# A two-layer hybrid decoder trunk: runs of sixteen products in the conv and gate projections, a later start of the second heads, and another room for the gated values

## The chip, the cores and the metric

The kernel runs on one core of a Trainium2 chip, in one launch. The metric is device time in microseconds (us), the median of several runs. The engines' names are those of the profile: PE is the matrix engine (PEld its weight loads), ACT the scalar engine, DVE the vector engine, POOL the general-purpose engine, SP the engine that issues most of the DMA transfers.

## What is computed

Input x has 256 tokens of 2048 features, in float32. Two layers follow each other. Cut to what matters here:

```python
for l in range(2):
    h = _rmsnorm(x, attn_norm_g[l])
    q, k, v, gate_b, gate_c, conv_in = split(h @ w_in[l])   # six parts of 1024 columns
    q, k = rmsnorm per 64 columns, with gains
    attn = diff_attention(q, k, v)       # 8 heads, two softmaxes each, one bias table
    attn = _rmsnorm(attn, subln_g[l]) * (1.0 - lam_init)
    conv = gate_b * _short_conv(gate_c * conv_in, conv_w[l])  # causal, 3 taps
    x = x + concatenate([attn, conv]) @ w_out[l]
    hm = _rmsnorm(x, mlp_norm_g[l]) @ w_up[l]                 # 8192 columns
    x = x + square(relu(hm)) @ w_down[l]
```

## The kernel before

**Products in three terms.** Every float32 operand is split into a part that PE's fast float32 form holds ("hi") and the rest ("lo"). A product of two operands is hi times hi, hi times lo and lo times hi. Weights come from memory as raw tiles of 128 x 1024 numbers (512 KB). For each, ACT writes the hi copy (`whi`, line 302) and DVE subtracts it from the raw tile (`wlo`, line 303). Three hi and three lo buffers exist (`wpool`), and four raw buffers in each mixer (`rpool`). `Weights.take` (line 357) hands out the next tile and has the following three made. In the MLP the same is done for the up weights (`uhi`, `ulo`, lines 818 and 819), from raw tiles of 1 MB (`uraw`, line 811), of which `upool` holds four.

**The mixer of a layer** (line 716) issues PE's work in this order: for each half of the heads q, k and v (16 contraction steps each, `linear`, line 373, 96 products of 512 columns); then four times gate-C and conv-in (`gc`, `ci`), then four times gate-B (`gb`), each of 256 output columns, all by `linear_t`; then four chunks of the output projection (`o`).

**`linear_t`** (line 392) turns the operands round: the weights are PE's stationary side, and the activations, hi and lo side by side (512 columns), move. For one weight tile of four contraction steps it issues eight products of `whi` with 512 moving columns ("wide" below) and then eight of `wlo` with the 256 hi columns ("narrow"). Sixteen contraction steps are four tiles: 64 products, in eight runs of eight. `up_part` (line 944), which makes the MLP's hidden columns, works the same way; when it is called with both halves of the contraction (the tiles `upw` and `upc`) it issues sixteen wide products from two weight tiles and then sixteen narrow ones. Called with one half (tile `up`, the MLP's first columns) it issues eight and eight.

**Background work.** PE's instructions run in the order in which the program issues them. Work of other stages is put between the products by steps: `Background.tick` (line 78) is called after a number of products, and each piece waiting in it counts down and goes on when its count is over. `linear` steps after six products. `linear_t` steps whenever k is odd, which is after every four products: 16 steps in a call. The order on ACT, DVE, POOL and SP is laid down when the program is built, by a planner with its own model of times; some instructions are kept in program order (`late`).

**Attention** (line 584) is such a piece. Four heads make up a half. A head computes scores in two banks (`sc`, line 604, eight products), DVE adds the bias and takes the maximum (610), ACT exponentiates (619), DVE joins the two softmaxes (630). After 10 x pace steps PE transposes (`ptp`, 635), after 4 x pace more it multiplies with the values (`av`, 646 and 648). The next head begins 8 x pace steps after the one before. 12 x pace steps after the last head's `av` the result is transposed in two goes, two steps apart (`atp`, 677), and ACT and DVE move each go into the tile `cat` (681 and 682). pace is 1 for the first half of the heads and 2 for the second. The call at line 763 starts a half 3 + 6 x half steps after its v projection, so the second half begins 9 steps into the first `gc`. All of `sc`, `ptp`, `atp` and some other small tiles take turns in three PSUM banks (`ps`, tag "bank").

**Gate and rooms.** `gate` (line 709) joins the two parts of a `gb` accumulator, multiplies them with the convolution's result into `y`, a tile of the shared pool `nat` (six buffers), and splits `y` into `cat` (lines 705 and 706). The masked keys `kL`, 8 KB per partition, lie in the pool `biasp` beside the bias table (16 KB); they are last read by the last head's scores. The mixer's pools are given up at its end, and the MLP's pools take their place in memory, `upool` first (4 x 8 KB); its tiles can be loaded as soon as whatever lay there has been read for the last time.

Of the kernel before, what the change touches and what calls it, by code (L numbers as in the profile page):

```python
# [9 lines left out]
F32 = mybir.dt.float32  # L10
F32R = mybir.dt.float32r
# [4 lines left out]
P = 128  # L16
DEPTH = 2
D = 2048
S = 256
NT = S // P  # L20
AW = 1024
# [8 lines left out]
WC = 256  # L30
KG = 4
# [14 lines left out]
def bucket_selector():  # L46

    import numpy as np

    d = np.arange(REL) - (P - 1)  # L50
    exact = NB // 2
    n = np.maximum(d, exact).astype(np.float64)
    large = exact + (np.log(n / exact) / math.log(MAXD / exact) * (NB - exact)).astype(np.int64)
    b = np.where(d < exact, d, np.minimum(large, NB - 1))
    b = np.where(d < 0, NB, b)
    return (np.arange(NB + 1)[:, None] == b[None, :]).astype(np.float32)


class Background:
# [46 lines left out]
def trunk(ctx: ExitStack, tc: tile.TileContext, x, w_in, w_out, conv_w, q_norm_g, k_norm_g,  # L106
# [8 lines left out]
    nat = ctx.enter_context(tc.tile_pool(name="nat", bufs=6))  # L115
# [10 lines left out]
    def bank(name):  # L126
        return ps.tile([P, CH], F32, tag="bank", name=name)
# [4 lines left out]
    work = Background()  # L132
# [56 lines left out]
    def tap(l, i, k):  # L189
        j = (l * 3 + i) * (AW // P) + k  # L190
        return gains[:, j:j + 1]
# [82 lines left out]
    class Parts:  # L274


        def __init__(self, pool, tag, name):
            self.make = lambda: pool.tile([P, 2, KG, S], F32R, tag=tag, name=name)
            self.ap = None
            self.ready = False  # L280
# [111 lines left out]
    def linear_t(name, acts, weights):  # L392

        acc = mm.tile([P, 2, 2, S], F32, tag="mm2", name=name)
        nk = len(acts) * KG
        for k0 in range(0, nk, 4):
            hi, lo = weights.take()  # L400
            a = acts[k0 // KG]
            while not a.ready:
                work.tick()
            for part, wt in ((0, hi), (1, lo)):
                for k in range(k0, k0 + 4):
                    for f in range(2):
                        fs = slice(f * P, (f + 1) * P)
                        nc.tensor.matmul(  # L408
                            acc[:, f, 0] if part else acc[:, f], wt[:, k % 4, fs],
                            a.ap[:, 0, k % KG] if part else a.ap[:, :, k % KG],  # L410
                            start=(part == 0 and k == 0), stop=(part == 1 and k == nk - 1),
                            skip_group_check=True)
                    if k % 2:
                        work.tick()
        return acc

    def joined(acc, name):

        low = nat.tile([P, 2, S], F32, tag="wide", name=f"{name}l")
        nc.scalar.activation(low, acc[:, :, 1], AF.Copy)  # L420
        whole = nat.tile([P, 2, S], F32, tag="wide", name=f"{name}w")
        nc.vector.tensor_add(whole, acc[:, :, 0], low)
        return whole
# [266 lines left out]
    def conv(l, q, u, cv, norm):  # L690

        for i in range(2):
            k = q * 2 + i
            nc.scalar.activation(cv[:, k], u[:, i], AF.Copy, scale=tap(l, 2, k))
            for back in (1, 2):
                nc.vector.scalar_tensor_tensor(
                    cv[:, k, back:], u[:, i, :S - back], tap(l, 2 - back, k),
                    cv[:, k, back:], op0=ALU.mult, op1=ALU.add)
        pair = cv[:, q * 2:q * 2 + 2]
        nc.gpsimd.tensor_tensor(pair, pair, norm.bc(1), op=ALU.mult)  # L700
# [5 lines left out]
        nc.vector.tensor_sub(lo, value, hi.bitcast(F32))  # L706
        dst.ready = j == 1

    def gate(q, acc, cv, dst):
        g = joined(acc, f"gb{q}")  # L710
        y = nat.tile([P, 2, S], F32, tag="wide", name=f"y{q}")
        nc.vector.tensor_mul(y, g, cv[:, q * 2:q * 2 + 2])
        in_parts(dst, q % 2, y)


    def mixer(l, norm, loads):

        with ExitStack() as scope:
            biasp = scope.enter_context(tc.tile_pool(name="biasp", bufs=1))
            tmp = scope.enter_context(tc.tile_pool(name="tmp", bufs=3))  # L720
            rpool = scope.enter_context(tc.tile_pool(name="rpool", bufs=RAW))
            bpool = scope.enter_context(tc.tile_pool(name="bpool", bufs=8))
            weights = Weights(rpool)
            setup = None
            if l == 0:
                setup = setup_loads(bpool.tile([P, 2 * KG * S], F32, tag="b", name="setup"))
            for half in range(2):
                for part in range(3):
                    weights.straight(w_in[l], 0, D // P, part * AW + half * CH)
            for q in range(AW // WC):  # L730
                for part in (4, 5):
                    weights.turned(w_in[l], part * AW + q * WC)
            for q in range(AW // WC):
                weights.turned(w_in[l], 3 * AW + q * WC)
            for n in range(D // CH):
                weights.straight(w_out[l], 0, D // P, n * CH)
            loads(weights)

            bias = biasp.tile([P, 2 * NH, S], F32, tag="bias", name="bias")
            work.start(load_bias(l, bpool, bias, setup), 10)  # L740
            hT = norm.tiles
            cat = [Parts(bpool, "b", f"cat{l}{i}") for i in range(4)]
            work.start(norm.factors(), 1)
            kL = biasp.tile([P, 2, 4, S], F32R, tag="kL", name=f"kL{l}")
            for m, r in enumerate(HALF):
                nc.gpsimd.memset(kL[HALF[1 - m], m].bitcast(F32), 0.0)
            for half in range(2):
                h0 = 4 * half
                acc = linear(f"q{l}{half}", hT, weights)
                r = norm.r  # L750
                qT = bpool.tile([P, 2, 4, S], F32R, tag="b", name=f"qT{l}{half}")
                work.start(qk_norm(acc, r, q_parts(qT), q_gain[:, l:l + 1], f"q{l}{half}"))
                acc = linear(f"k{l}{half}", hT, weights)
                kT = bpool.tile([P, 2, 4, S], F32R, tag="b", name=f"kT{l}{half}")
                work.start(qk_norm(acc, r, k_parts(kT, kL), k_gain[:, l:l + 1], f"k{l}{half}"))
                acc = linear(f"v{l}{half}", hT, weights)
                v = bpool.tile([P, 2, NT, CH], F32R, tag="b", name=f"v{l}{half}")
                for t in range(NT):
                    nc.scalar.activation(v[:, 0, t], acc[:, t], AF.Copy, scale=r[:, t:t + 1])
                    nc.vector.scalar_tensor_tensor(v[:, 1, t], acc[:, t], r[:, t:t + 1],  # L760
                                                   v[:, 0, t].bitcast(F32),
                                                   op0=ALU.mult, op1=ALU.subtract)
                work.start(attention(l, qT, kT, kL, v, h0, cat[half], bias, tmp,
                                     1 + half), 3 + 6 * half)
            cv = bpool.tile([P, AW // P, S], F32, tag="b", name=f"cv{l}")
            for q in range(AW // WC):
                acc = linear_t(f"gc{l}{q}", hT, weights)
                u = joined(acc, f"gc{l}{q}")
                nc.gpsimd.tensor_tensor(u, u, norm.bc(2), op=ALU.mult)
                acc = linear_t(f"ci{l}{q}", hT, weights)  # L770
                i = joined(acc, f"ci{l}{q}")
                nc.vector.tensor_mul(u, i, u)
                conv(l, q, u, cv, norm)
            for q in range(AW // WC):
                acc = linear_t(f"gb{l}{q}", hT, weights)
                gate(q, acc, cv, cat[2 + q // 2])

            mnorm = Norm(1, l)
            for n in range(D // CH):
                acc = linear(f"o{l}{n}", cat, weights)  # L780
                for t in range(NT):
                    nc.vector.tensor_add(xs[n][:, t], acc[:, t], xs[n][:, t])
                work.start(mnorm.chunk(n, 2))
        return mnorm
# [5 lines left out]
    def mlp(l, mnorm, last):  # L790
# [3 lines left out]
        SEVEN = [i for i in SEVEN_AT if i < 2 * BLK]  # L794
        mT = mnorm.tiles
        with ExitStack() as scope:
            upool = scope.enter_context(tc.tile_pool(name="upool", bufs=4))
            fpool = scope.enter_context(tc.tile_pool(name="fpool", bufs=2))
            dpool = scope.enter_context(tc.tile_pool(name="dpool", bufs=3))
            spool = scope.enter_context(tc.tile_pool(name="spool", bufs=1))  # L800
# [3 lines left out]
            weights = Weights(upool)  # L804
# [197 lines left out]
            for i in range(NP):  # L1002
# [15 lines left out]
                for c in range(2):  # L1018
                    if i < LAG:
                        acc = bank("upw").rearrange("p (h s) -> p h s", h=2)  # L1020
                    else:
                        acc = column_bank()
# [10 lines left out]
                    if j >= 0 and c == 0:  # L1033
                        b11, b21, b22 = weights.take()
                        t1, t3 = weights.take()
                        f = fs[j]
# [5 lines left out]
                    elif j >= 0:  # L1042
                        t2, t4 = weights.take()
                        f = fs[j]
# [223 lines left out]
```

## Time and profile before

| | |
|---|---|
| median of 3 runs | 2133.45 us (2132.67 to 2133.55) |
| the profiled execution | 2133.02 us |
| its span, first to last instruction | 2131.2 us |
| granted clock of PE | 1.00 throughout |
| PE busy | 2125.1 us |
| DVE / ACT / POOL busy | 1693.9 / 1349.2 / 165.6 us |
| PE's products | 10925 |
| gc, ci, gb of layer 0 | from 156.06 us to 300.71 us |
| gc, ci, gb of layer 1 | begin about 1059 us later |

Times in the rows that follow are us from the start of the span. A timeline row has the start, how long it lasted, the engine, the source line, the operation, out<-in by the program's tile names, the shape (partitions x elements) and the number of instructions that were merged into it; products overlap in the pipe, so the pace is the distance of one row's start from the next one's, not the duration. A bracket at the end is idle time before the row and what ended it. A row of waits has the waiting engine and tile, what it waited for, us in total, times, longest us. A row of the chain has the start, us, and what. A row of DMA issues has the count, the size, and the median us from issue to landing. A row of windows has the stretch, its length, the busy time of PE, PEld, DVE, ACT and POOL with counts, the clock, the DMA engines' busy share and GB/s.

### The profile page before, as it was taken

The page shows a single profiled execution, that of the slowest core. Times are in us where ns is not written, and L with a number is a line of the kernel's source. Part 1 is how long each engine was busy: PE and PEld are TensorE (multiplying, and loading weights), DVE is VectorE, ACT ScalarE, POOL GpSimd, SP SyncE. Part 2 cuts the span into 40 slices and gives each one's busy share as a digit, 9 for nine tenths or more (in the row PEclk, how much of TensorE's full clock was granted, in tenths as well). Part 3 has the DMA queues.
Part 4 walks back from the last instruction along what each step waited for, and adds up shares of the span by engine and source line. Part 5 has one row for each costly group of instructions (what it writes and reads, how often), then busy time and mean ns, then how long its engine had stood idle before and what let it go on. Part 6 is the DMA issues. An engine that isn't in the chain of part 4 may idle for free.

```text
span 2131.2 us, 29207 instructions
## 1 busy us (share of the span) xinstructions
PE 2125.1 (100%) x10925; PEld 1818.4 (85%) x10925; DVE 1693.9 (79%) x2316; ACT 1349.2 (63%) x1776; POOL 165.6 (8%) x226
## 2 busy tenths in 40 slices
PE   9999999999999999999999999999999999999999
PEld 8888888888888888888888888888888888888887
DVE  6778655798888888798766786557988888888986
ACT  6666545677777777656565665446777777675654
POOL 3110100000000000011111101000000000000110
PEclk9999999999999999999999999999999999999999
DMA  8555766677777777788656558656877777777983
GB/s 271 178 166 167 252 193 187 206 252 229 230 236 229 233 235 229 255 297 287 216 170 182 163 162 264 188 178 211 259 231 233 232 235 229 236 229 259 319 297 112
DMA packets 298255, 476.01 MB, mean 223 GB/s; under 512 B 12708, under 2 KB 193782, under 8 KB 298113
## 3 DMA queue, kind: packets, MB, share of 16 engines
q1 hardware_dynamic: 269120, 406.76, 60.5%
q0 software_dynamic: 28800, 67.24, 10.1%
q8 instruction: 85, 1.39, 0.3%
q14 instruction: 58, 0.47, 0.1%
q10 hardware_dynamic: 192, 0.15, 0.0%
HBM read 440.52 MB, written 33.58 MB: 222 GB/s over the span
## 4 chain that ended last, share of the span: by engine, by line
PE 99%; ACT 1%; DVE 0%; issue 0%; DVEq 0%; ACTq 0%
PE upc L955 31%; PE pr L998 14%; PE dn L1079 8%; PE o L386 8%; PE ci L408 4%; PE gb L408 4%; PE k L386 4%; PE q L386 4%; PE v L386 4%; PE gc L408 4%; PE dn L1161 2%; PE dn L998 2%; PE pr1r L998 1%; PE pr0r L998 1%; PE up L955 1%; PE upw L955 1%
## 5 line engine op out<-in xcount | busy, mean ns | idle before, releaser
L303 DVE TENSOR_TENSOR wlo<-raw,whi 128x1024 fp32r<-128x1024 f32 x274 | 343.0, 1252 | 217.8 <-ACT whi L302 213.6
L302 ACT ACTIVATE whi<-raw 128x1024 fp32r<-128x1024 f32 x274 | 290.4, 1060 | 303.3 <-PE o L386 73.6
L955 PE MATMUL upc<-nT,uhi 128*128 128x512 f32 x1920 | 454.7, 389 | 0.0
L955 PEld LDWEIGHTS upc<-nT,uhi 128*128 128x128 f32 x1920 | 360.3, 188 | 74.7
L819 DVE TENSOR_TENSOR ulo<-uraw,uhi 128x1024 fp32r<-128x1024 f32 x256 | 311.9, 1222 | 119.1 <-ACT f L987 91.4
L818 ACT ACTIVATE uhi<-uraw 128x1024 fp32r<-128x1024 f32 x256 | 270.5, 1057 | 159.9 <-PE upc L955 137.5
L955 PEld LDWEIGHTS upc<-nT,ulo 128*128 128x128 f32 x1920 | 246.2, 191 | 9.3
L955 PE MATMUL upc<-nT,ulo 128*128 128x256 f32 x1920 | 249.1, 283 | 0.0
L1079 PE MATMUL dn<-whi,fb 128*128 128x512 f32 x528 | 166.1, 389 | 0.0
L386 PE MATMUL o<-whi,cat 128*128 128x512 f32 x512 | 159.5, 390 | 0.0
L302 ACT ACTIVATE whi<-uraw 128x1024 fp32r<-128x1024 f32 x66 | 70.1, 1062 | 94.0 <-PE dn L1079 77.5
L1079 PEld LDWEIGHTS dn<-whi,fb 128*128 128x128 f32 x528 | 99.1, 188 | 20.6
L844 ACT ACTIVATE b2h<-draw 128x1024 fp32r<-128x1024 f32 x81 | 85.9, 1061 | 45.9 <-PE pr L998 41.3
L386 PEld LDWEIGHTS o<-whi,cat 128*128 128x128 f32 x512 | 96.2, 188 | 19.7
L965 ACT ACTIVATE ev<-upc 128x512 f32<-128x512 f32 x120 | 72.0, 600 | 54.1 <-PE upc L955 54.1
L1079 PE MATMUL dn<-wlo,fb 128*128 128x512 f32 x264 | 102.7, 389 | 0.0
L303 DVE TENSOR_TENSOR wlo<-uraw,whi 128x1024 fp32r<-128x1024 f32 x66 | 80.7, 1223 | 24.8 <-ACT whi L302 24.5
L844 ACT ACTIVATE t24h<-t 128x1024 fp32r<-128x1024 f32 x81 | 86.2, 1064 | 22.2 <-PE pr L998 15.8
L845 DVE TENSOR_TENSOR b2l<-draw,b2h 128x1024 fp32r<-128x1024 f32 x81 | 98.5, 1217 | 1.7 <-ACT b2h L844 1.7
L845 DVE TENSOR_TENSOR t24l<-t,t24h 128x1024 fp32r<-128x1024 f32 x81 | 98.7, 1219 | 1.3
L386 PE MATMUL o<-wlo,cat 128*128 128x512 f32 x256 | 99.6, 389 | 0.0
L845 DVE TENSOR_TENSOR t13l<-t,t13h 128x1024 fp32r<-128x1024 f32 x81 | 98.7, 1219 | 1.1
(408 smaller groups left out, 4153.3 us busy)
## 6 DMA issues: line engine op xcount, KB each, us to landing
uraw<-in_w_up_dram SPq DMA_DIRECT2D x128, 1024.0 KB, 6.2
raw<-in_w_in_dram SPq DMA_DIRECT2D x191, 512.0 KB, 3.8
draw<-in_w_down_dram SPq DMA_DIRECT2D x170, 512.0 KB, 5.2
uraw<-in_w_down_dram SPq DMA_DIRECT2D x66, 512.0 KB, 5.3
raw<-in_w_out_dram SPq DMA_DIRECT2D x64, 512.0 KB, 3.6
hid0p<-f POOLq DMA_DIRECT2D x20, 512.0 KB, 3.6
raw<-in_w_down_dram SPq DMA_DIRECT2D x10, 1024.0 KB, 5.1
fb<-hid0p POOLq DMA_DIRECT2D x20, 512.0 KB, 7.4
```

The source lines that it names most:

```text
L302: pair = (nc.scalar.activation(hi, raw, AF.Copy), nc.vector.tensor_sub(lo, raw, hi.bitcast(F32)))
L303: nc.vector.tensor_sub(lo, raw, hi.bitcast(F32)))
L386: nc.tensor.matmul(acc[:, t], a.ap[:, pa, k % KG, t * P:(t + 1) * P], (hi, lo)[pw][:, j], start=(k == 0 and n == 0), stop=(k == nk - 1 and ...
L408: nc.tensor.matmul(acc[:, f, 0] if part else acc[:, f], wt[:, k % 4, fs], a.ap[:, 0, k % KG] if part else a.ap[:, :, k % KG], start=(part ...
L818: pair = (nc.scalar.activation(hi, src, AF.Copy), nc.vector.tensor_sub(lo, src, hi.bitcast(F32)))
L819: nc.vector.tensor_sub(lo, src, hi.bitcast(F32)))
L844: keep(nc.scalar.activation(hi, src, AF.Copy))
L845: keep(nc.vector.tensor_sub(lo, src, hi.bitcast(F32)))
L955: nc.tensor.matmul(acc[:, 0] if part else acc, wt[part][:, k], a.ap[:, 0, k % KG] if part else a.ap[:, :, k % KG], start=(part == 0 and kh ...
L965: nc.scalar.activation(ev, acc, AF.Copy)
L998: nc.tensor.matmul(prods[n], f[:, pa, a], b[pw], start=(start and m == 0), stop=(stop and m == 2))
L1079: nc.tensor.matmul(prods[p], f[:, pa, 2 * k + t], b[pw][:, n], start=(p in starts and k == 0 and m == 0), stop=(stop and k == 1 and m == 2))
```

## The change

Three things change, in one diff.

- `linear_t` takes two weight tiles at a time and issues sixteen wide products from their hi parts and then sixteen narrow ones from their lo parts. The steps stay at 16 a call, but in a pair of runs they now come after 2, 6, 8, 10, 14 and 16 wide products and after 8 and 16 narrow ones.
- The second half of the heads starts 12 steps after its v projection instead of 9.
- `kL` gets a pool of its own, `kpool`, placed behind `biasp` so that the bytes stay where they were. When the masked keys are done, a tile `ys` takes that room and holds the gated values of all four `gb` blocks. The MLP's `upool` becomes two pools of two buffers, `upa` and `upb`, used by turns, two tiles of each.

```diff
+class Turns:
+    def __init__(self, *pools):
+        self.pools, self.n = pools, 0
+
+    def tile(self, *args, **kw):
+        self.n += 1
+        return self.pools[(self.n - 1) // 2 % 2].tile(*args, **kw)
...
         nk = len(acts) * KG
-        for k0 in range(0, nk, 4):
-            hi, lo = weights.take()
-            a = acts[k0 // KG]
-            while not a.ready:
-                work.tick()
-            for part, wt in ((0, hi), (1, lo)):
-                for k in range(k0, k0 + 4):
+        for k0 in range(0, nk, 8):
+
+            tiles = [weights.take() for _ in range(2)]
+            for part in range(2):
+                for k in range(k0, k0 + 8):
+                    a = acts[k // KG]
+                    while not a.ready:
+                        work.tick()
+                    wt = tiles[(k - k0) // 4][part]
                     for f in range(2):
...
-                    if k % 2:
+                    if k % 4 == 3 or (part == 0 and k % 2 == 0):
                         work.tick()
...
-    def gate(q, acc, cv, dst):
+    def gate(q, acc, cv, dst, y):
         g = joined(acc, f"gb{q}")
-        y = nat.tile([P, 2, S], F32, tag="wide", name=f"y{q}")
...
             biasp = scope.enter_context(tc.tile_pool(name="biasp", bufs=1))
+            kpool = scope.enter_context(tc.tile_pool(name="kpool", bufs=1))
...
-            kL = biasp.tile([P, 2, 4, S], F32R, tag="kL", name=f"kL{l}")
+            kL = kpool.tile([P, 2, 4, S], F32R, tag="kL", name=f"kL{l}")
...
                 work.start(attention(l, qT, kT, kL, v, h0, cat[half], bias, tmp,
-                                     1 + half), 3 + 6 * half)
+                                     1 + half), 3 + 9 * half)
...
+            ys = kpool.tile([P, AW // WC, 2, S], F32, tag="kL", name="ys")
             for q in range(AW // WC):
                 acc = linear_t(f"gb{l}{q}", hT, weights)
-                gate(q, acc, cv, cat[2 + q // 2])
+                gate(q, acc, cv, cat[2 + q // 2], ys[:, q])
...
-            upool = scope.enter_context(tc.tile_pool(name="upool", bufs=4))
+            upool = Turns(scope.enter_context(tc.tile_pool(name="upa", bufs=2)),
+                          scope.enter_context(tc.tile_pool(name="upb", bufs=2)))
```

## The prediction

> **What bounds the kernel now.** First the page: which engine is busy, and who ends the chain.
>
> ```profile
> span 2131.2 us, 29207 instructions
> PE 2125.1 (100%) x10925; PEld 1818.4 (85%) x10925; DVE 1693.9 (79%) x2316; ACT 1349.2 (63%) x1776; POOL 165.6 (8%) x226
> PE 99%; ACT 1%; DVE 0%; issue 0%; DVEq 0%; ACTq 0%
> ```
>
> PE never rests and is 99% of the chain that ended last. So only two things can move the time: the spacing of PE's products, or an idle stretch that PE gets or loses. The second view, the waits of PE, lists all the idle time there is:
>
> ```profile
> PE sc L604 <- DVE cat L682: 1.2, 2, 0.6
> PE warm L160 <- DVE mhalf L152: 1.1, 1, 1.1
> ```
>
> The second line is the start of the program, which the change leaves alone. The first is one wait per layer. The third view, PE's timeline at the beginning of gate-C's first block (gc, layer 0), shows where it lies:
>
> ```profile
> 156.06 1.98 PE L408 MATMUL gc<-nT,whi 128*128 128x512 f32 x8
> 157.87 1.12 PE L408 MATMUL gc<-nT,wlo 128*128 128x256 f32 x8
> 158.82 1.09 PE L408 MATMUL gc<-nT,whi 128*128 128x512 f32 x4
> 159.75 0.60 PE L677 MATMUL atp<-ident,an 128*128 128x128 f32 x4
> 160.10 1.17 PE L408 MATMUL gc<-nT,whi 128*128 128x512 f32 x4
> 161.11 0.64 PE L408 MATMUL gc<-nT,wlo 128*128 128x256 f32 x4
> 161.59 0.60 PE L677 MATMUL atp<-ident,an 128*128 128x128 f32 x4
> 161.94 0.72 PE L408 MATMUL gc<-nT,wlo 128*128 128x256 f32 x4
> 162.50 1.09 PE L408 MATMUL gc<-nT,whi 128*128 128x512 f32 x4
> 163.43 0.22 PE L604 MATMUL sc<-kT,qT 128*128 128x128 f32 x1
> 164.26 0.38 PE L604 MATMUL sc<-kT,qT 128*128 128x256 f32 x1 [0.61 <-DVE cat L682]
> ...
> 165.18 1.09 PE L408 MATMUL gc<-nT,whi 128*128 128x512 f32 x4
> ```
>
> The two atp lines are the first heads' last transposes, put in at steps 5 and 7 of this block (a step, a tick of the code, now follows every four products). The second heads' scores begin at step 9. There are three score banks, so the second score product takes the bank of the first atp and waits until DVE has emptied it:
>
> ```profile
> 163.47 0.74 DVE L682 SCALAR_TENSOR_TENSOR cat<-atp,s_gain,cat 128x512 fp32r<-128x512 f32 x1
> 164.12 1.22 DVE L303 TENSOR_TENSOR wlo<-raw,whi 128x1024 fp32r<-128x1024 f32 x1
> ```
>
> It ends at 163.47 + 0.74 = 164.21 and PE goes on at 164.26; the line below it is DVE's part in making a weight tile.
>
> **Part 1: the second heads three steps later.** An undisturbed set of scores, one head later in the same layer:
>
> ```profile
> 176.37 0.39 PE L604 MATMUL sc<-kT,qT 128*128 128x128 f32 x2
> ...
> 177.28 1.07 PE L408 MATMUL ci<-nT,whi 128*128 128x512 f32 x4
> ```
>
> From first score to next gc or ci product: 177.28 - 176.37 = 0.91 us undisturbed, 165.18 - 163.43 = 1.75 at the first. The wait costs 0.84 us per layer (more than the 0.61 listed as idle, since what was in the pipe runs empty), 1.7 us for two. Does it go? The new step 12 stands ten wide products into the second run. From 156.06: fourteen wide products (3.2), atp (0.35), two wide (0.54) and eight narrow (0.95), atp (0.35), eight narrow (1.04), ten wide (2.3) make 164.8. The bank is free at 164.21 if ACT and DVE keep their order, so there is 0.6 us to spare. The second atp's bank is wanted only by the next head, 16 steps on. I take the whole 1.7; the ends are 0 (DVE does the eviction after the weight tile that follows it, 1.22 us later) and 1.7. What is late next: by the waits view, nothing; the other scores, transposes and value products show no wait now and keep their distances of 20 and 8 steps. The second heads end three steps later, at step 116 of the 192 that gc, ci and gb have, and their result is read only after those.
>
> **Part 2: runs of sixteen.** Each block (linear_t, 24 of them: gc, ci, gb, four each, two layers) issues 64 products as eight runs now, and as four after. Count and operands stay. What a change of run costs is read where both forms exist. In gb's first runs, and in upw, the MLP's first columns, which already go in sixteens:
>
> ```profile
> 255.86 2.00 PE L408 MATMUL gb<-nT,whi 128*128 128x512 f32 x8
> 257.70 1.11 PE L408 MATMUL gb<-nT,wlo 128*128 128x256 f32 x8
> ```
>
> ```profile
> 402.55 3.82 PE L955 MATMUL upw<-nT,uhi 128*128 128x512 f32 x16
> 406.20 2.08 PE L955 MATMUL upw<-nT,ulo 128*128 128x256 f32 x16
> 408.12 1.09 PE L955 MATMUL upw<-nT,uhi 128*128 128x512 f32 x4
> ```
>
> Start to start: eight wide 1.84, sixteen 3.65, so the second eight take 1.81: the first products of a wide run behind a narrow one are slower, 0.03 us in all. Narrow: eight take 0.95 (157.87 to 158.82 above), sixteen 1.92, which gives some 0.01 to 0.02 back. The chain has it without rounding:
>
> ```profile
> 256.02 44.69 PE gb L408 x256
> ...
> 402.71 11.13 PE upw L955 x64
> ...
> 422.16 5.54 PE upc L955 x32
> ```
>
> A block takes 44.69 / 4 = 11.17 us in eights and 11.13 in sixteens: 0.04 less, times 24 = 1.0 us. With the 5.54 of a pair of runs that follows other wide products it would be 0.09, times 24 = 2.2; 0 is the other end. I take 1.0, as upw alone has sixteens behind sixteens.
>
> The Trainium skill ("TensorE: Matmul & The Clock Gate", Back-to-back issue gap) gives the distance of two products as moving columns / 2.4 plus 2.5 ns, whatever went before, and by that the length of a run is worth nothing. The trace has 3.65 / 16 = 228 ns in long runs and 1.84 / 8 = 230 in short ones, where that rule has 216 in both: it doesn't hold here to the ns that this part is about. By it the sum below would be 1.7; it stays a rival.
>
> The steps stay 16 per block but shift. The second heads' transposes (steps 32, 48, ...), value products (40, 56, ...) and first atp (112) now stand between a narrow and a wide run, where now they cut a wide run:
>
> ```profile
> 179.15 1.09 PE L408 MATMUL ci<-nT,whi 128*128 128x512 f32 x4
> 180.08 0.49 PE L635 MATMUL ptp<-ident,s 128*128 128x128 f32 x3
> 180.32 1.18 PE L408 MATMUL ci<-nT,whi 128*128 128x512 f32 x4
> 181.34 1.10 PE L408 MATMUL ci<-nT,wlo 128*128 128x256 f32 x8
> ```
>
> Four wide products take 0.93 before the transposes and 1.02 behind them: a slow start again. Placed where a slow start (0.03) is due anyway, the two can merge: 9 places, 2 layers, 0 to 0.03 each, 0 to 0.5 us; I take 0.3.
>
> **Weights two at a time.** The 96 tiles of a layer's mixer input, in blocks that now take two before sixteen products, still have three buffers. In a pair of runs (3.65 + 1.92 = 5.57 us) the first tile's wide half is free after 1.84, and its successor is wanted one pair and 1.84 later: 5.57 us for an ACT pass (1.06, the whi rows below) and a DVE pass (1.22, the wlo row above). upw and upc live with the same buffers and the same runs and show no wait. Cost 0. Behind a late weight pass stand, on ACT and DVE, evictions of the blocks and of the heads; PE needs a block's accumulator back a whole block (11 us) later.
>
> **Part 3: gated values in the masked keys' room.** y moves from the shared pool to the room of kL; the same multiply, no copy. The room is free after the last head's scores (step 60 of 192), the first gate comes after step 144: no wait, cost 0. What moves is a transfer. The MLP's first four up-weight loads now start as soon as the heads' rooms are free:
>
> ```profile
> 232.92 3.56 SPq L811 DMA_DIRECT2D uraw<-in_w_up_dram  x3
> 236.57 3.93 SPq L343 DMA_DIRECT2D raw<-in_w_in_dram  x1
> ```
>
> ```profile
> 247.30 1.06 ACT L302 ACTIVATE whi<-raw 128x1024 fp32r<-128x1024 f32 x1 [1.72 <-DMA raw<-in_w_in_dram]
> 251.46 1.06 ACT L302 ACTIVATE whi<-raw 128x1024 fp32r<-128x1024 f32 x1 [3.09 <-DMA raw<-in_w_in_dram]
> ```
>
> The w_in load issued behind three of them at 236.57 let ACT go on only at 247.30, 10.7 us later; and ACT waited 1.72 us for it and 3.09 for the next.
>
> ```profile
> raw<-in_w_in_dram SPq DMA_DIRECT2D x191, 512.0 KB, 3.8
> ```
>
> Such a load takes 3.8 us as a rule, so three 1 MB loads ahead of it cost 6.9. PE did not wait: the buffers covered it. With two pools the first pair lies over the bias alone and can still go in this stage; the second lies over kL's room and waits for the last gated value:
>
> ```profile
> 305.73 0.68 DVE L706 TENSOR_TENSOR cat<-y,cat 128x512 fp32r<-128x512 f32 x1
> ```
>
> ```profile
> 300.70:393.00 92.30, 92.30 (x426) 76.77 (x425) 52.18 (x57) 45.01 (x64) 0.00 (x0) 1.00 0.52 158
> ```
>
> So two of the four 1 MB loads go to about 305.73 + 0.68 = 306.4, into the output projection, where the DMA engines are 52% busy (the 0.52), and are wanted at 402 (the upw row). Behind them on SP stand the w_out loads. A w_out tile serves twelve wide products, 12 x 0.228 = 2.7 us; with four raw buffers three others are in hand, some 8 us. Two loads ahead would cost 2/3 of 6.9 = 4.6: they fit. Cost 0, and ACT's waits in gc and ci shrink. If the cover were gone, each us too much is one us of PE per layer.
>
> **The sum.** 1.7 + 1.0 + 0.3 = 3.0 us off the profiled execution's 2133.0 (span 2131.2 and 1.8 around it): **2130.0**. The profiled execution is 0.4 below the median of the runs (2133.45); the result's own median may stand as much above. A measurement of this kernel can tell about 0.2% (4.3 us) from no change, so this is a gain inside that bound.
>
> **Rivals.**
>
> *A. The wait stays.* ACT and DVE are served in an order fixed beforehand; if another weight pass goes ahead of the first atp's eviction, it ends 1.22 us later, at 165.4 instead of 164.21, against 164.8, and the change doesn't do what it says. For it: the first atp was issued at 159.75 and is emptied only at 164.21, so ACT or DVE runs behind there. Against: 0.6 us in hand, and the weights are asked for in pairs, so less often. Time: 2133.0 - 1.3 to 2133.0 - 2.0, about **2131.7**.
>
> *B. Run length is worth nothing.* Every product keeps its own spacing, and the slow start comes from elsewhere, say from the weight tile that changes there. Then part 1 alone is left: 2133.0 - 1.7 = **2131.3**. Against: upw changes its tile in mid-run, after eight products, and its second eight are the quicker ones. The rule of the Trainium skill ("TensorE: Matmul & The Clock Gate", Back-to-back issue gap) would have it so.
>
> *C. Slower: the up-weight loads hit a thinner cover.* In sixteens the second tile of a pair is wanted directly behind the first one's wide run, 0.95 us sooner than now. Place: gc/ci when the first pair of loads goes, or the output projection at 306. There two loads would have to delay a raw tile beyond some 8 us. Three did so by 6.9 in the trace: PE held, but ACT's 3.09 shows the edge is not far. Price: two layers times the excess; past 1.5 us of excess per layer the gain of 3.0 is gone. With 3 us too much in each: 2130.0 + 6 = **2136**. Against: two loads at a time, no longer three and one.
>
> *D. More.* With the 2.2 of part 2 and 0.5 for merged starts: 2133.0 - 4.4 = **2128.6**.
>
> **How the numbers follow.** Forecast (2129.2 to 2130.8) 0.60, A 0.13, B 0.08, C 0.12, D 0.07. The range runs from D's 2128.6 to 2133.0, which takes in A and B and the lightest cases of C. Faster by over 0.2% (below 2129.2): D and a little of the forecast, 0.09. Slower by over 0.2% (above 2137.7): the upper half of C, 0.05. Within: 0.86.
>
> **What would show it.** PE's waits: the sc line gone (A: it stays, at 0.1 to 0.6). The chain: a gb stretch of 256 products at 44.5 instead of 44.69 (B: 44.69; D: 44.3). PE's timeline: ptp and av between wlo and whi of gc or ci, and less than 1.02 us over 0.93 behind them. SP's timeline: two uraw loads in gc/ci, two near 306, in layer 1 near 1366. C would show as a PE wait on whi or wlo in gc, ci, gb or o. The forecast is wrong if PE shows any new wait of a us or more, or if stages that the diff doesn't touch change in length.

## The result, and the profile after

| | before | after |
|---|---|---|
| median | 2133.49 us (22 runs, 2132.35 to 2134.83) | 2130.61 us (22 runs, 2130.24 to 2131.02) |
| profiled execution, its span | 2133.02, 2131.2 us | 2131.02, 2129.2 us |

The ratio is 0.9987 (95% interval 0.9981 to 0.9992): 2.9 us less, where 3.0 was predicted; the median lies 0.6 above the 2130.0 that was forecast, inside the range, and the profiled execution 1.0 above it. Two things in the table need an answer. The two profiled executions differ by 2.0 us, not 2.9. And the runs of before spread over 2.5 us, those of after over 0.8.

The page of the changed kernel: the span, PE's share and the chain.

```profile
span 2129.2 us, 29221 instructions
PE 2124.3 (100%) x10925; PEld 1819.3 (85%) x10925; DVE 1685.0 (79%) x2316; ACT 1350.6 (63%) x1776; POOL 160.8 (8%) x226
PE 100%; DVE 0%; DVEq 0%; issue 0%
```

PE's waits in the changed kernel are one line, the start of the program. The sc line is gone:

```profile
PE warm L171 <- DVE mhalf L163: 1.1, 1, 1.1
```

PE's timeline at the beginning of gc, layer 0 (lines of the changed file; L421 is linear_t's product, L617 the scores, L690 the first heads' last transposes):

```profile
156.29 3.34 PE L421 MATMUL gc<-nT,whi 128*128 128x512 f32 x14
159.46 0.60 PE L690 MATMUL atp<-ident,an 128*128 128x128 f32 x4
159.82 0.72 PE L421 MATMUL gc<-nT,whi 128*128 128x512 f32 x2
160.37 1.11 PE L421 MATMUL gc<-nT,wlo 128*128 128x256 f32 x8
161.32 0.60 PE L690 MATMUL atp<-ident,an 128*128 128x128 f32 x4
161.67 1.20 PE L421 MATMUL gc<-nT,wlo 128*128 128x256 f32 x8
162.71 2.46 PE L421 MATMUL gc<-nT,whi 128*128 128x512 f32 x10
165.01 0.39 PE L617 MATMUL sc<-kT,qT 128*128 128x128 f32 x2
...
165.93 1.55 PE L421 MATMUL gc<-nT,whi 128*128 128x512 f32 x6
```

The scores come at 165.01 and take 0.92 us. DVE's timeline shows the bank free at 163.03 + 0.74 = 163.77, 1.2 us ahead:

```profile
163.03 0.74 DVE L695 SCALAR_TENSOR_TENSOR cat<-atp,s_gain,cat 128x512 fp32r<-128x512 f32 x1
```

The chain has the blocks of gb, all four together, and the unchanged upw:

```profile
255.27 44.53 PE gb L421 x256
...
401.82 11.13 PE upw L972 x64
```

44.53 / 4 = 11.13 a block, as in upw. SP's timeline has the up loads in pairs, the first when the bias is free, the second behind the last gated value:

```profile
205.63 0.99 SPq L828 DMA_DIRECT2D uraw<-in_w_up_dram  x2
208.11 8.13 SPq L354 DMA_DIRECT2D raw<-in_w_in_dram  x4
```

```profile
305.60 0.99 SPq L828 DMA_DIRECT2D uraw<-in_w_up_dram  x2
307.71 8.48 SPq L354 DMA_DIRECT2D raw<-in_w_out_dram  x4
```

For the kernels of this study, the length of the stages in the trace, from the first product of one to the first of the next, in us (layer 0 / layer 1, one number where both agree within 0.01):

| kernel | first gc | the other seven of gc, ci | gb | o |
|---|---|---|---|---|
| before | 13.79 | 86.01 | 44.69 | 89.75 |
| after | 12.94 | 85.89 | 44.53 | 89.76 |
| part 1 alone | 12.96 | 86.20 / 87.91 | 44.69 | 89.75 |
| part 2 alone | 13.63 | 91.81 / 90.74 | 44.53 | 89.75 |
| part 3 alone | 13.79 | 86.01 | 44.69 | 89.75 |
| parts 1, 2 | 12.94 | 89.60 / 88.63 | 44.53 | 89.76 |
| parts 1, 3 | 12.96 | 86.03 | 44.69 | 89.75 |
| parts 2, 3 | 13.63 | 85.77 | 44.53 | 89.76 |
| after, one pool of four | 12.94 | 85.89 | 44.53 | 95.22 / 94.25 |
| after, gated values in the shared pool | 12.94 | 85.89 | 44.53 | 89.76 |
| after, start at step 13 | 12.91 | 85.80 | 44.53 | 89.75 |
| after, every second pair turned | 12.95 | 86.34 | 44.51 / 44.45 | 89.72 |
| before, second execution | 13.78 | 86.65 / 86.00 | 44.69 | 89.75 |
| before, third execution | 13.78 | 86.32 / 87.23 | 44.69 | 89.75 |

What lies between the first gc of layer 0 and that of layer 1, beside these four columns, differs from before's by less than 0.05 us. What lies ahead of the first gc varies from one execution to the next, by up to 0.8 us among these traces (in after's execution the first gc came 0.23 late). Before to after, each layer has 0.85 less in the first gc, 0.12 in the next seven blocks and 0.16 in gb: 1.13 a layer, 2.26 in all. So the traces show 2.3 of the 2.9.

### The profile page after: what moved, and what is told of

It reads as the page before. It is cut to its first block, busy times and chain, and to the rows that moved or that the text cites. A ratio compares the mean times of both kernels' runs of the same rounds, so it can differ in the third digit from the quotient of the medians.

```text
span 2129.2 us, 29221 instructions
## 1 busy us (share of the span) xinstructions
PE 2124.3 (100%) x10925; PEld 1819.3 (85%) x10925; DVE 1685.0 (79%) x2316; ACT 1350.6 (63%) x1776; POOL 160.8 (8%) x226
## 4 chain that ended last, share of the span: by engine, by line
PE 100%; DVE 0%; DVEq 0%; issue 0%
PE upc L972 31%; PE pr L1015 14%; PE dn L1096 8%; PE o L397 8%; PE ci L421 4%; PE gc L421 4%; PE gb L421 4%; PE k L397 4%; PE v L397 4%; PE q L397 4%; PE dn L1178 2%; PE dn L1015 2%; PE pr1r L1015 1%; PE pr0r L1015 1%; PE up L972 1%; PE upw L972 1%
## 5 line engine op out<-in xcount | busy, mean ns | idle before, releaser
L314 DVE TENSOR_TENSOR wlo<-raw,whi 128x1024 fp32r<-128x1024 f32 x274 | 331.9, 1223 | 221.9 <-ACT whi L313 150.3
```

The lines of the kernel that those rows point to most:

```text
L314: nc.vector.tensor_sub(lo, raw, hi.bitcast(F32)))
```

## The experiments

The theory after the result: the wait for the first atp's bank gives most, the runs of sixteen the rest, and the rooms give nothing. The rival: the rooms matter too, by way of the up loads, in a way that no trace of before had shown.

**Part 1 alone.**

```diff
-                                     1 + half), 3 + 6 * half)
+                                     1 + half), 3 + 9 * half)
```

> Part 1 alone: the second heads start after 12 steps, runs stay at eight, rooms as before. Theory (the wait for the first atp's bank is the largest part of the gain): the scores come at 165.3, a us after the bank is free, the sc line leaves PE's waits, 1.7 us off, 2131.8 against 2133.5. Rival (the wait only moves, since ACT and DVE empty the bank later as well): the sc line stays and the time is within 0.4 of before.

Measured 2132.25 (11 runs, 2131.08 to 2134.28), ratio 0.9994 (0.9985 to 1.0003). The sc line is gone, as expected, and the first gc is 0.83 shorter. But PE has a new wait, in the seventh block after it in layer 1; PE's waits in this kernel:

```profile
PE ci L408 <- ACT whi L302: 1.3, 1, 1.3
PE warm L160 <- DVE mhalf L152: 1.1, 1, 1.1
```

ACT's timeline there shows what ACT waited for, twice, longer than in the trace of before (1.72 and 3.09):

```profile
1307.13 1.06 ACT L302 ACTIVATE whi<-raw 128x1024 fp32r<-128x1024 f32 x1 [4.21 <-DMA raw<-in_w_in_dram]
1311.45 1.06 ACT L302 ACTIVATE whi<-raw 128x1024 fp32r<-128x1024 f32 x1 [2.69 <-DMA raw<-in_w_in_dram]
```

In this execution, of 2133.41 us, the late weight tiles cost 2.05 us: the seven blocks are 0.17 and 1.88 longer than in parts 1 and 3. Of the 1.7 that the start saved, nothing is left in it. The fastest run, 2131.08, has no room for such a wait, so the tile cannot be late in every run; that the spread of 3.2 us comes of it is likely, but no second trace of this kernel was taken.

**Part 2 alone.** `linear_t` as after the change; start at step 9, rooms as before.

> Part 2 alone: runs of sixteen, start at step 9, rooms as before. The second heads' scores then come two wide products into the second run, at about 163.3, so the sc wait stays at 0.4 to 0.9 per layer. All four up-weight loads stand in a row on SP's queue in gc/ci in this kernel. Theory (runs gain 0.3 us per layer, as the trace of the changed kernel shows, and four loads at once eat more than the cover, rival C of the prediction): gain 0.6, loss 1 to 3 per layer, so 2134 to 2139, with a PE wait on whi or wlo in gc or ci. Rival (the cover is wide enough): 2132.5 to 2133.3 and no wait but sc.

Measured 2142.67 (5 runs, 2139.98 to 2144.85), ratio 1.0042 (1.0029 to 1.0054): 9.2 slower than before, more than expected. PE's waits:

```profile
PE ci L410 <- ACT whi L302: 7.4, 2, 4.3
...
PE sc L606 <- DVE cat L684: 1.0, 2, 0.5
```

The planner put all four up loads in a row here, as SP's timeline shows, and PE waited 4.3 us in layer 0 and 3.1 in layer 1 for the weights behind them.

```profile
231.86 6.57 SPq L813 DMA_DIRECT2D uraw<-in_w_up_dram  x4
```

The wait costs more than its length; PE's timeline and the windows with the granted clock (PE, PEld, DVE, ACT and POOL busy, then the clock) show why:

```profile
250.35 3.58 PE L410 MATMUL ci<-nT,whi 128*128 128x512 f32 x8 [4.28 <-ACT whi L302]
253.76 2.07 PE L410 MATMUL ci<-nT,wlo 128*128 128x256 f32 x16
```

```profile
246.00:250.30 4.30, 0.06 (x1) 0.00 (x0) 0.00 (x0) 1.06 (x1) 0.93 (x1) 0.98 1.06 376
250.30:252.00 1.70, 1.65 (x4) 1.37 (x5) 1.49 (x2) 1.06 (x1) 0.00 (x0) 0.50 0.31 111
252.00:254.00 2.00, 2.00 (x8) 1.57 (x7) 0.96 (x1) 1.10 (x2) 0.00 (x0) 0.61 0.62 195
```

Behind the wait the granted clock is 0.50, and eight wide products take 253.76 - 250.35 = 3.41 us instead of 1.84.

**Part 3 alone.** Rooms and pools as after, runs of eight, start at step 9.

> Part 3 alone: gated values in the keys' room, up tiles in two pools, runs of eight, start at step 9. Theory (rooms only move transfers; PE did not wait for them): within 0.3 us of before, 2133.2 to 2133.8, sc wait as before. Rival (in some executions before PE did wait for a weight tile behind the up loads, which a single trace doesn't show, and that is why the median fell by 0.6 us more than the two traces differ, and why the runs of before spread over 2.5 us and those after over 0.8): 0.6 us off, and the spread of its runs falls to 1 us.

Measured 2132.97 (11 runs, 2132.32 to 2133.35), ratio 0.9996 (0.9988 to 1.0005). 0.5 less than the 2133.46 of before beside it, and a spread of 1.0 instead of 2.6; its trace has the two sc waits and no wait for a weight tile in gc, ci or gb. The interval takes in no change, but both signs point to the rival.

**Parts 1 and 2, without the rooms.**

> Parts 1 and 2 without part 3: runs of sixteen, start at step 12, y in the shared pool, one pool of four up tiles, so three and one up loads go in gc/ci as before. Theory (C: with sixteens the second tile of a pair is wanted 0.95 us sooner, and the loads already had ACT waiting 3.09 us): a PE wait of 0.4 to 1.5 us per layer on whi in gc or ci, 2131.4 to 2133.6. Rival (part 3 does nothing for the time): 2130.6, no PE wait.

Measured 2138.25 (10 runs, 2136.76 to 2141.43), ratio 1.0023 (1.0014 to 1.0033): 7.6 slower than the whole change and 4.8 slower than before, beyond what either theory expected. Nothing but the rooms is missing. SP's, ACT's and PE's timelines in layer 0 have the whole chain:

```profile
232.96 5.28 SPq L813 DMA_DIRECT2D uraw<-in_w_up_dram  x3
238.34 3.23 SPq L343 DMA_DIRECT2D raw<-in_w_in_dram  x1
241.61 1.23 SPq L813 DMA_DIRECT2D uraw<-in_w_up_dram  x1
```

```profile
248.95 1.06 ACT L302 ACTIVATE whi<-raw 128x1024 fp32r<-128x1024 f32 x1 [3.52 <-DMA raw<-in_w_in_dram]
253.09 1.06 ACT L302 ACTIVATE whi<-raw 128x1024 fp32r<-128x1024 f32 x1 [3.08 <-DMA raw<-in_w_in_dram]
```

```profile
250.06 2.11 PE L410 MATMUL ci<-nT,whi 128*128 128x512 f32 x8 [1.12 <-ACT whi L302]
254.20 2.11 PE L410 MATMUL ci<-nT,whi 128*128 128x512 f32 x8 [2.03 <-ACT whi L302]
```

A w_in load issued at 238.34 behind three up loads lets ACT go on at 248.95, and PE at 250.06. The second tile, 254.20, is the other half of the same run of sixteen: it is wanted as soon as the first half's eight products are done, and so waits again. Layer 1 has two more such waits, 5.3 us in all in this execution, the shortest of the ten. The same place in before's trace had ACT waiting 3.09 us and PE not at all, but not by much: the tile was ready at 251.46 + 1.06 = 252.52, and PE took it at 253.06.

```profile
253.06 2.00 PE L408 MATMUL ci<-nT,whi 128*128 128x512 f32 x8
```

That is 0.54 us in hand, and runs of sixteen want the tile 0.95 us sooner. Here the loads also landed later than in that trace.

**Where the loads go, and how many in a row.** Two kernels, each with one half of part 3. All of the change with one pool:

```diff
-            upool = Turns(scope.enter_context(tc.tile_pool(name="upa", bufs=2)),
-                          scope.enter_context(tc.tile_pool(name="upb", bufs=2)))
+            upool = scope.enter_context(tc.tile_pool(name="upool", bufs=4))
```

> All of the change, but the up tiles in one pool of four: all four 1 MB loads then wait for the last gated value and go in a row in the output projection, near 306. Theory (what counts is how many up loads stand in a row ahead of the weights that PE wants): two in a row had ACT waiting 2.7 us for a w_out tile there and PE none; two more add 5.4 us, of which PE's tiles in hand cover some 3, so a PE wait of 1 to 4 us per layer in o: 2133 to 2138. By the prediction's own cover (8 us against 9.2) it would be 1.2 per layer, 2133. Rival (the harm in the kernels without rooms came from the place, gc and ci, and not from the number in a row): 2130.6, no PE wait.

Measured 2140.39 (5 runs, 2139.22 to 2141.61), ratio 1.0032 (1.002 to 1.0044): 9.8 slower than the whole change and beyond the 2138 that was expected. SP issues four up loads at 305.00, gc, ci and gb are as after, and the whole loss lies in o. SP's timeline, PE's timeline behind the loads, and the windows with the clock:

```profile
305.00 7.14 SPq L827 DMA_DIRECT2D uraw<-in_w_up_dram  x4
```

```profile
323.52 0.51 PE L397 MATMUL o<-whi,cat 128*128 128x512 f32 x1 [2.52 <-ACT whi L313]
324.78 0.51 PE L397 MATMUL o<-wlo,cat 128*128 128x512 f32 x1 [0.76 <-DVE wlo L314]
```

```profile
325.00:327.00 2.00, 2.00 (x7) 1.57 (x7) 1.32 (x2) 1.59 (x2) 0.00 (x0) 0.65 0.56 139
327.00:329.00 2.00, 2.00 (x7) 1.41 (x6) 1.04 (x1) 0.00 (x0) 0.00 (x0) 0.50 0.64 207
329.00:331.00 2.00, 2.00 (x14) 1.82 (x13) 0.71 (x1) 1.79 (x3) 0.00 (x0) 0.99 0.96 348
```

3.3 us of waiting, then some 3.4 us at half the clock, which costs half of that: about 5.0 of the 5.46 us by which o is longer in this layer.

And all of the change with the gated values left in the shared pool:

```diff
...
+        y = nat.tile([P, 2, S], F32, tag="wide", name=f"y{q}")
...
-            ys = kpool.tile([P, AW // WC, 2, S], F32, tag="kL", name="ys")
```

> All of the change, but the gated values in the shared pool as before: both pairs of up loads go in gc/ci, the first near 205 when the bias is free, the second near 233. Theory (number in a row): no PE wait on weights, within 0.4 us of the changed kernel's 2130.6. Rival (the up loads must leave gc/ci, so the gated values' new room is what pays): a PE wait on whi in ci as without the rooms, 2133 to 2138.

Measured 2130.80 (11 runs, 2130.26 to 2131.18), ratio 0.9986 (0.9977 to 0.9995), no different from the whole change. SP issues the second pair at 233.36, in the place where three in a row did the harm. ACT waits 5.06 us behind it, PE not at all:

```profile
233.36 1.00 SPq L828 DMA_DIRECT2D uraw<-in_w_up_dram  x2
```

```profile
245.32 1.06 ACT L313 ACTIVATE whi<-raw 128x1024 fp32r<-128x1024 f32 x1 [5.06 <-DMA raw<-in_w_in_dram]
```

So the number in a row decides, not the place, and it is the two pools of up tiles that pay, not the gated values in the keys' room. (Both kernels keep `kL` in a pool of its own; no run has the two pools with `kL` back in `biasp`.)

The rows give the size. From the first up load's issue to ACT's pass over the first weight tile loaded behind them went by 11.6 us (after, 305.60 to 317.24) and 12.0 us (this kernel) with two in a row, 14.4 us (before, 232.92 to 247.30) and 16.0 us (parts 1 and 2) with three, and 17.4 us with four, in gc/ci as in o (231.86 to 249.24 and 305.00 to 322.41). That is some 2.8 us for each load more.

**Parts 1 and 3, runs of eight.**

> Parts 1 and 3, runs of eight. Sizes part 2 where nothing else waits. Theory (by the traces a pair of runs saves 0.02 us, some of it lost again behind scores): 0.4 to 0.8 us slower than the changed kernel, 2131.0 to 2131.4. Rival (prediction: 1.3 us with the merged starts): 2131.9. Rival (length of a run is worth nothing): 2130.6.

Measured 2131.33 (11 runs, 2131.08 to 2132.15), ratio 0.9989 (0.9980 to 0.9998): the runs of sixteen are worth 0.7 us, within the theory's range, and its fastest run is slower than the slowest of the changed kernel (2131.02). The table has 0.16 for gb's four blocks, 0.14 for the next seven and 0.02 for the first, times two.

**Parts 2 and 3, start at step 9.**

> Parts 2 and 3, start at step 9: what part 1 is worth where no weight is late. Theory (the scores at 163.3 meet a bank that is emptied at 163.8 to 164.2): a sc wait of about 0.5 us idle in each layer as in the kernel with part 2 alone, and what is lost besides as the pipe refills, so 1.0 to 1.8 us slower than the changed kernel, 2131.6 to 2132.4. Rival (with runs of sixteen the eviction comes early enough anyhow): 2130.6 and no sc wait.

Measured 2131.74 (11 runs, 2131.51 to 2131.99), ratio 0.9990 (0.9980 to 0.9999): the start is worth 1.1 us beside the other two, again with no run of one as fast as any of the other. The table has the same: 0.69 a layer in the first gc, less 0.12 that the seven blocks after it lose by the later start. PE waits 0.5 us per layer for the bank:

```profile
163.31 0.36 PE L617 MATMUL sc<-kT,qT 128*128 128x256 f32 x1 [0.52 <-DVE cat L695]
```

**A step later.** `3 + 10 * half`, all else as after.

> All of the change, start at step 13: scores then come after fourteen wide products, the transposes and value products after two wide ones, instead of between a narrow and a wide run. Theory (by the trace the slow start begins anew wherever it is cut, so merging saves nothing): within 0.3 us of the changed kernel, 2130.3 to 2130.9. Rival (prediction: merged starts save up to 0.5): 2131.0 to 2131.1.

Measured 2130.53 (11 runs, 2130.04 to 2130.89), ratio 0.9985 (0.9976 to 0.9994), the changed kernel's time within its spread. Transposes between two runs are no better than transposes that cut a wide one: the trace even has 0.12 a layer less with the cut (12.91 and 85.80 against 12.94 and 85.89).

**Every second pair of runs turned round**, to look for a faster version.

```diff
-            for part in range(2):
+            for part in ((0, 1), (1, 0))[k0 // 8 % 2]:
...
-                            start=(part == 0 and k == 0), stop=(part == 1 and k == nk - 1),
+                            start=(part == 0 and k == 0), stop=(part == 0 and k == nk - 1),
```

> All of the change, and the second pair of runs of each block turned round: wide, narrow, narrow, wide, so that a block changes width twice instead of four times. Theory: 0.02 us for each of 48 changes to wide saved, 24 are left, 0.5 us off, 2130.1; but the narrow half of a tile is then free only 0.95 us before the end of the narrow run and its successor wanted 0.95 us after the start of the next, 1.9 us for a DVE pass of 1.22, and where DVE is late PE waits up to a us in each block: 2130 to 2142. Rival (three buffers cover that too): 2130.1 and no wait.

Measured 2131.84 (11 runs, 2131.28 to 2133.11), ratio 0.9993 (0.9984 to 1.0001): 1.2 slower than the changed kernel. gb is 0.02 to 0.08 shorter per layer, but the other blocks after the first are 0.45 longer. PE's waits list 0.3 us for wlo in ci, in two places; what the rest is stays open.

**The kernel before, twice more.** One execution each, with a profile.

> The kernel before, once more with a profile. Its runs spread over 2.5 us, those of the kernels with the new rooms over 1. Theory (in some executions PE waits for a weight tile behind the three up loads): if this execution is a long one (2134 or more), its trace has a PE wait on whi or wlo in ci or gb beside the two sc waits; if it is a short one, it has none. Rival (the spread comes from the start of the program): no such wait, and the first q product comes later by as much.

> The same, one more execution, for the same two theories: a long one has a PE wait on a weight tile in ci or gb, a short one has none; or the difference lies ahead of the first q product.

The two took 2133.81 and 2134.61 us. PE's timeline has a wait in each that the trace of before has not, in ci, of the first one in layer 0, of the second in layer 1:

```profile
253.71 2.11 PE L408 MATMUL ci<-nT,whi 128*128 128x512 f32 x8 [0.38 <-ACT whi L302]
```

```profile
1313.77 2.12 PE L408 MATMUL ci<-nT,whi 128*128 128x512 f32 x8 [0.95 <-ACT whi L302]
```

Each has ACT waiting for a w_in load just ahead. The first of the two falls short of the 2134 that was set as long, and has a wait all the same, the smaller one. The first gc product came at 156.18 and 156.13 us, against 156.06 in the trace of before, so what lies ahead of it explains 0.1 us at most. The kernel before stands on the edge: in some executions PE waits, in others not, and the execution that was profiled first was one without, with 0.54 us in hand. Why the same load lands a us later in one execution than in another, these traces do not show.

| left out of the change | median, us | worth beside the others, us |
|---|---|---|
| nothing | 2130.61 | |
| part 1, the later start | 2131.74 | 1.1 |
| part 2, runs of sixteen | 2131.33 | 0.7 |
| part 3, rooms and pools | 2138.25 | 7.6 |

## Why the prediction was right, and where it was not

The time and its place inside the 0.2% bound were right, and the signs that the prediction named came: no sc line, gb at 44.53, pairs of up loads near 206 and 306. That a gain of this size could not be told from no change did not hold: the interval ends at 0.9992. And that 2.9 came so near to 3.0 is in part luck, as two errors met. Step by step:

- **Part 1, 1.7 us.** Right for the kernel as it stood: the first gc is 0.83 shorter in part 1 alone, times two. Beside the runs of sixteen it is worth 1.1, since with those alone the scores already met a shorter wait (13.63 against 13.79) and the later start makes the seven blocks behind it 0.12 longer (85.89 against 85.77). The new step came 1.2 us after the bank was free, where 0.6 was worked out, because DVE emptied it sooner (163.77).
- **Part 2, 1.0 us from upw's blocks.** gb came out as predicted, 0.16 a layer. The eight blocks of gc and ci gave 0.16 a layer in place of 0.32. Added up start to start over these blocks of layer 0, the narrow products gave back what gb says (0.10, gb's four blocks 0.06), but the wide ones gained 0.25 (59.73 us in parts 1 and 3, 59.48 after) where twice gb's 0.22 would be 0.43. The heads' products cut the long runs there, and behind a cut the slow start begins anew; with the cuts in other places, in parts 2 and 3, the same products took 59.39. That the cuts are the whole of it is not shown. Measured 0.7 in all.
- **Merged starts, 0.3 us.** Nothing: a step later, where the transposes cut a wide run again, costs nothing (2130.53), and is 0.24 us shorter in the trace.
- **Rival B**, that a run's length is worth nothing, fell with the 0.7. The Trainium skill's rule ("TensorE: Matmul & The Clock Gate", Back-to-back issue gap) makes the gap follow from N alone, by which the runs of sixteen would be worth nothing; the trace does not agree, with 230 against 228 ns a wide product, and the measurement decides.
- **Part 3, cost 0.** This is the step that was mis-sized. "PE did not wait: the buffers covered it" was read from one execution; in others of the same kernel PE waits 0.38 and 0.95 us there, and in the one that was read it had 0.54 us in hand. Part 3 alone measured 0.5 less, and that is most of the 0.6 by which the medians differ more than the first two traces. The two errors: the sum had 0.7 too much in parts 1 and 2 (3.0 against the traces' 2.3) and 0.6 too little here.
- **Rival C** named the mechanism: up loads in a row, and a second tile of a pair wanted sooner. It had the place (ci, whi), and it is what the change would do without part 3. Its bound of "some 8 us" of cover, worked out for o, was too wide: by it four loads in a row, 9.2 us, should have cost 1.2 a layer in o, and cost 5.46 and 4.49. In gc and ci, where a tile serves 1.84 + 0.95 = 2.8 us and three in hand make the same 8, the 6.9 us of three loads should have cost nothing, and cost 3.7 and 2.7 with runs of sixteen. The price was too low as well: 6.9 us counts from the w_in load's own issue at 236.57, but SP had turned to the up loads at 232.92, and ACT's pass came 14.4 us after that. Two in a row cost PE nothing in either place, as predicted. How much of the cover ACT and DVE eat before a tile reaches PE was not worked out.

## What to carry to other kernels

A wait that an engine's buffers absorb is no proof of room to spare: when a feeding engine shows DMA waits of several us, take more than one trace, and look at the spread of the runs, before calling it covered. A change of order that wants an operand even a us sooner should be costed together with the transfers queued ahead of that operand. Big early loads do least harm split up. Here two in a row cost PE nothing in any of three places (near 205, 233 and 306). Three in a row cost 0.5 us in all with runs of eight and 7.6 with runs of sixteen. Four in a row cost 9.8 in o, and 10.9 in gc and ci (2142.67 for part 2 alone against 2131.74 for parts 2 and 3).

## What the runs showed of the hardware

- **A long wait of PE is paid twice.** In four places the granted clock fell to 0.50, for 3.41 us each time: behind waits of 4.28 and 3.13 us (part 2 alone, layers 0 and 1), and behind 2.52 and 0.76 us and 1.84 and 0.76 us, each with one product between them (one pool of four, layers 0 and 1). Wide products then went at half their pace, 427 ns apart in place of 227. The windows of the last case have PE busy for 1.35 of the 3.41 us before the clock fell; in the other three it was 1.33, 1.17 and 0.00.

```profile
1383.74:1387.15 3.41, 1.35 (x5) 0.56 (x3) 2.03 (x3) 1.83 (x4) 0.00 (x0) 1.00 1.04 404
1387.15:1390.57 3.42, 2.88 (x7) 2.30 (x8) 2.47 (x3) 2.35 (x4) 0.00 (x0) 0.50 0.67 211
```

Behind waits of 1.12 and 2.03 us with eight products between them (parts 1 and 2) the clock stayed at 1.00, and each eight wide products took 2.11 us in the rows, as behind 0.38 us in the second execution of before. Where the limit lies between these, no run shows. The Trainium skill ("TensorE: Matmul & The Clock Gate", What's actually happening) describes a clock halved after an idle window of about 3.4 us and given back after a busy one. The traces agree on the halving and on the 3.41 us until it is given back; they do not on the idle window, which had PE busy for up to 1.35 us.
- **The slow start of a wide run.** Behind narrow products the first five wide ones lay 233, 236, 228, 233 and 230 ns apart and the next five 226 or 227 (after's trace, from 162.71), 0.03 us in all. Behind the heads' transposes the first took 0.31 us and the next three 233 to 236 ns (before's trace, from 180.32). Putting one on the other saves nothing that the medians show (2130.53 against 2130.61).
